# Feed-forwards by seven products in four of eight pairs, with four summed tiles and a fixed TensorE order

## The chip, the core and the metric

The kernel runs on one core of a Trainium2 chip. The metric is the device time of one execution in microseconds (us); the time before is the median of three runs. The engines are TensorE (PE in the profile; its weight loads are PEld), VectorE (DVE), ScalarE (ACT), GpSimd (POOL) and SyncE (SP), which only starts DMA transfers. Each has a queue of its own that it works through in order, and they meet by semaphores.

## The reference

One layer of an encoder on 256 tokens of width 2048, all in float32: a first feed-forward, a mixing layer (convolution and spatial gating side by side), cross-attention into 256 memory tokens, a second feed-forward, and a final norm. The change concerns the feed-forwards:

```python
def swiglu_ffn(h, w_in, w_out):
    gate, up = jnp.split(h @ w_in, 2, axis=-1)
    return (jax.nn.silu(gate) * up) @ w_out

h = rms_norm(x, ffn1_norm)
x = x + 0.5 * swiglu_ffn(h, ffn1_w_in, ffn1_w_out)
...
h = rms_norm(x, ffn2_norm)
x = x + 0.5 * swiglu_ffn(h, ffn2_w_in, ffn2_w_out)
```

`w_in` is 2048 x 11264 and `w_out` 5632 x 2048.

## The kernel before

**Numbers in two parts.** Every matmul is in fp32r. Both factors are split into a rounded high part and the remainder, the low part, and three matmuls are made: high x high, high x low, low x high. The activations are split once. Each weight tile (128 x 1024, 512 KB) is split as it comes: a load by SP's queue into a `raw` buffer, a cast on ScalarE (L397, the high part), a subtraction on VectorE (L398, the low part), both into a buffer `hl`. `parts` does this for the feed-forwards, with three rotating `hl` buffers and two more called `ring` (three in the first feed-forward, one of them called `more`).

**Groups.** The first product of a feed-forward, h @ w_in, goes in 11 groups of 512 gate and 512 up columns (`NG` is 11). Group 0 is written out in `run`; groups 1 to 10 call `group`. A group runs over 16 tiles k of 128 rows, taken as 8 pairs p (tiles 2p and 2p+1). A pair is a 256 x 256 by 256 x 1024 product, cut in two each way, and it is done in one of two ways, which `PATTERNS` spells:

- `C`, by `eight`: eight block products of 128 x 128 by 128 x 512, so 24 matmuls (`by_two` makes 12 for each tile).
- `S`, by `seven`: seven block products of sums and differences, as in Strassen's scheme, so 21 matmuls (`three` makes the 3 of one product). It needs sums of weight blocks, which VectorE makes (L470, L471, L477, L484), and sums of activation blocks, the `forms`, made once by `sides` in group 0. Its products are issued in the order 5, 7, 6, 1, 2, 3, 4. Their weights are split in four steps: `sums` for 5 and 7, the first tile for 6 and 1, the second tile for 2 and 3, and 512 columns more for 4.

The pattern is SCSCSCCC: three pairs by seven.

**Banks.** A group takes all eight PSUM banks, one for each product name 1 to 7 and one, 8, that only the `C` pairs use. When the last `S` pair of a group is done, `joins_sevens` adds products 1, 5, 6 and 7 into four SBUF accumulators: ScalarE copies bank 1 (L521) and VectorE makes four additions (L522 to L525). These free the banks 5, 7, 6 and 1, with which the next group begins. Products 2, 3, 4 and 8 gather on through the `C` pairs; at the end of the group VectorE adds them (L550, four times) and `give` applies the silu on ScalarE (L510) and the products on VectorE (L512).

**Summed tiles.** To spare VectorE, some tiles of `C` pairs get their low part in another way (`summed`): the raw tile is loaded, ScalarE writes the negative high part (L426) and the high part (L427), and a DMA from POOL's queue adds the raw tile from HBM onto the negative high part (L428). `SUMMED` names them: tiles 2, 7 and 13 of a group. Their raw load stands in SP's queue (L425). Two buffer sets alternate (`hl_s` and `more`, or two called `hl_s`); from group 8 of the second feed-forward on there is one, and the tiles are 2 and 10 (`ALONE`). The next tile of a buffer set is begun right after the cast that follows the tile's use (`self.next`).

**Other parts.** The product with `w_out` of the first feed-forward is done by `out_block`, with the same `seven` and `eight`. `turn` makes four transposes on TensorE and splits what they give, so that the result of the first product can be used by the second.

**What sets the order.** The program is written in source order. A planner takes it to pieces at build time: it goes through a modelled timeline and gives each engine the order of its instructions, by when they can run, so products of different pairs may be mixed. `tc.issue_after(ins)` ties what is issued inside its block, on the engine of `ins` alone, behind `ins` in that engine's order.

Of the kernel before, what the change touches and what calls it, by code (L numbers as in the profile page):

```python
# [36 lines left out]
PATTERNS = ("SCSCSCCC", "SCSCSCCC")  # L37

SUMMED = ((2, 7, 13), (2, 7, 13))
ALONE = (2, 10)  # L40

# [37 lines left out]
def layer(ctx: ExitStack, tc: tile.TileContext, a: dict):  # L79
# [220 lines left out]
    def turning(o, c, sink):  # L300

        def go():
            tp = pa.tile([P, 2, T], F32, name="aux")
            for k in range(2):
                for t in range(2):
                    nc.tensor.transpose(  # L306
                        out=tp[:, k, t * P:(t + 1) * P], in_=o[:, t, c + k * P:c + (k + 1) * P], identity=ident
                    )
            sink(tp)
        return go  # L310
# [5 lines left out]
    def three(acc, x, hi, lo, first, last):  # L316

        nc.tensor.matmul(acc, lhsT=x[0], rhs=hi, start=first, stop=False)  # L318
        nc.tensor.matmul(acc, lhsT=x[0], rhs=lo, start=False, stop=False)  # L319
        nc.tensor.matmul(acc, lhsT=x[1], rhs=hi, start=False, stop=last)  # L320

    def by_two(acc, x, hi, lo, k, first, last):

        cols = [slice((g + 1 - k % 2) % 2 * G, (g + 1 - k % 2) % 2 * G + G) for g in range(2)]
        for t in range(2):
            s = slice(t * P, (t + 1) * P)
            for g in range(2):  # L330
                nc.tensor.matmul(acc[t][g], lhsT=x[:, 0, s], rhs=hi[:, cols[g]], start=(t, g) in first, stop=False)  # L331
                nc.tensor.matmul(acc[t][g], lhsT=x[:, 0, s], rhs=lo[:, cols[g]], start=False, stop=False)  # L332
            for g in range(2):
                nc.tensor.matmul(acc[t][g], lhsT=x[:, 1, s], rhs=hi[:, cols[g]], start=False, stop=last)  # L334
# [7 lines left out]
    class FeedForward:  # L342
# [6 lines left out]
        def __init__(self, stack, tags, x_hl, gain, w_in, pattern, summed, w_out=None, pair=False):  # L349
# [34 lines left out]
            self.next = None  # L384
# [34 lines left out]
        def summed(self, at):  # L419
# [5 lines left out]
            nc.sync.dma_start(out=raw, in_=self.w_in[j, :, k])  # L425
# [38 lines left out]
        def seven(self, j, p, b, last):  # L464

            k = 2 * p
# [19 lines left out]
            three(b["4"], self.half(j, k + 1, 1), w[:, 0, lo], w[:, 1, lo], self.begins("4"), False)  # L486
# [5 lines left out]
        def eight(self, j, p, b, last, plain, between=None):  # L492
            for k in (2 * p, 2 * p + 1):
# [7 lines left out]
                by_two(acc, self.x(j, k), w[:, 0], w[:, 1], k, begin, last and k % 2 == 1)  # L501
# [18 lines left out]
        def joins_sevens(self, b, p1, u2, u4, u5):  # L520
            nc.scalar.copy(out=p1, in_=b["1"])  # L521
# [3 lines left out]
            nc.vector.tensor_tensor(out=u5, in0=u2, in1=b["5"], op=ALU.add)  # L525

        def group(self, j, r, after=()):
# [8 lines left out]
            n = len(self.pattern)  # L536
            for p, c in enumerate(self.pattern):
                if c == "S":
                    self.seven(j, p, b, p == self.spairs[-1])
                    if p == self.spairs[-1]:  # L540
                        self.joins_sevens(b, p1, u2, u4, u5)
                else:
                    late = p > self.spairs[-1] and len(after) > 0
                    self.eight(j, p, b, p == n - 1, late)
                    if p > self.spairs[-1] + 1:
# [110 lines left out]
        def turn(self, i):  # L656

            def go():
# [17 lines left out]
                turning(self.h[i // 2], i % 2 * 2 * P, both)()  # L676
# [13 lines left out]
    with ExitStack() as stack:  # L690
# [7 lines left out]
        def x_more(k):  # L698
# [4 lines left out]
            if k in (6, 9, 12):  # L703
                ff.sides(k // 3 - 2)
# [490 lines left out]
    with ExitStack() as stack:  # L1195
# [15 lines left out]
        def first_beside(k):  # L1211
            if k in (6, 9, 12):
                ff.sides(k // 3 - 2)
# [156 lines left out]
```

## Time and profile before

| | us |
|---|---|
| median of three runs | 2089.99 |
| lowest and highest | 2089.42, 2090.06 |
| the profiled execution | 2088.91 |
| its span, first to last instruction | 2087.1 |
| its TensorE busy | 2076.4 |
| its VectorE busy | 1622.5 |
| its ScalarE busy | 1174.4 |

In the profile a row of a timeline gives the start, the busy duration, engine, line, operation, what it writes and reads, the shape and the count; in square brackets stand the idle time before it and what ended that. Durations of instructions that follow each other overlap at their ends, so the time that a row of them takes is read from the distance of their starts. A table by stage gives for each stretch of time how long each engine was busy and with how many instructions. L331 to L334 are the matmuls of `by_two`, L318 to L320 those of `three`.

### The profile page before, as it was taken

How to read it: one execution, taken by the hardware profiler on the slowest of the kernel's cores; microseconds unless marked ns; L12 is line 12 of the kernel's file. 1: busy time of each engine (PE TensorE's matmuls, PEld its weight loads, DVE VectorE, ACT ScalarE, POOL GpSimd, SP SyncE). 2: the span in 40 equal slices, each digit the busy share in tenths (PEclk: the TensorE clock that was granted, in tenths of full speed). 3: DMA queues.
4: the chain of work that ended last, by engine and by line, in shares of the span. 5: the costliest groups of instructions: out<-in, count | busy, mean ns of one | idle time of the engine just before them, and what ended most of it. 6: DMA issues, size and time to landing. Idle time of an engine off the chain costs nothing.

```text
span 2087.1 us, 26730 instructions
## 1 busy us (share of the span) xinstructions
PE 2076.4 (99%) x9765; PEld 1739.0 (83%) x9765; DVE 1622.5 (78%) x2302; ACT 1174.4 (56%) x1470; POOL 66.0 (3%) x81
## 2 busy tenths in 40 slices
PE   9999999999999999999999999999999999999998
PEld 8888888888888888888888899888888888888886
DVE  7888888877777689989877666778888888787754
ACT  8665666555545554445764455566665655554443
POOL 0000000000000000000000000000000000000000
PEclk9999999999999999999999999999999999999999
DMA  9787778755566576655555543687777777556664
GB/s 366 246 263 246 232 223 263 230 182 192 188 203 234 180 238 199 186 179 187 180 196 192 184 160 124 200 291 224 237 236 253 222 217 230 169 166 203 195 192 152
DMA packets 122245, 441.30 MB, mean 211 GB/s; under 512 B 13569, under 2 KB 13953, under 8 KB 121729
## 3 DMA queue, kind: packets, MB, share of 16 engines
q1 hardware_dynamic: 113184, 407.08, 57.1%
q0 software_dynamic: 8352, 31.46, 8.1%
q8 instruction: 76, 1.25, 0.2%
q10 hardware_dynamic: 576, 1.06, 0.1%
q14 instruction: 57, 0.46, 0.1%
HBM read 437.44 MB, written 2.10 MB: 211 GB/s over the span
## 4 chain that ended last, share of the span: by engine, by line
PE 87%; issue 11%; POOL 1%; DMA 1%; ACT 0%; DVE 0%; DVEq 0%; POOLq 0%
PE acc L332 11%; PE acc L331 11%; PE acc L334 11%; PE acc L204 8%; PE acc L205 8%; PE acc L203 8%; PE acc L154 8%; PE acc L162 4%; PE acc L318 3%; PE acc L319 3%; PE acc L320 3%; PE aux L306 1%; PE aux L318 1%; PE aux L319 1%; PE aux L320 1%
## 5 line engine op out<-in xcount | busy, mean ns | idle before, releaser
L124 ACT CAST hl<-raw 128x1024 fp32r<-128x1024 f32 (+1 forms) x315 | 327.1, 1040 | 358.9 <-PE acc L205 191.9
L125 DVE TENSOR_TENSOR hl<-raw,hl 128x1024 fp32r<-128x1024 f32 (+1 forms) x315 | 381.2, 1212 | 165.0 <-ACT hl L124 163.6
L397 ACT CAST hl<-raw 128x1024 fp32r<-128x1024 f32 (+1 forms) x151 | 147.6, 988 | 117.3 <-PE acc L334 48.2
L398 DVE TENSOR_TENSOR hl<-raw,hl 128x1024 fp32r<-128x1024 f32 (+1 forms) x151 | 172.2, 1145 | 47.4 <-ACT hl L397 45.7
L398 DVE TENSOR_TENSOR hl<-spare,hl 128x1024 fp32r<-128x1024 f32 (+1 forms) x125 | 144.7, 1162 | 32.5 <-ACT hl L397 30.3
L397 ACT CAST hl<-spare 128x1024 fp32r<-128x1024 f32 (+1 forms) x125 | 124.3, 1002 | 66.4 <-PE acc L334 24.2
L332 PE MATMUL acc<-hl,x_hl 128*128 128x512 f32 x388 | 140.9, 390 | 0.1
L331 PE MATMUL acc<-hl,x_hl 128*128 128x512 f32 x388 | 135.7, 390 | 0.0
L334 PE MATMUL acc<-hl,x_hl 128*128 128x512 f32 x388 | 120.6, 390 | 0.0
L397 ACT CAST ring<-spare 128x1024 fp32r<-128x1024 f32 (+1 forms) x83 | 82.1, 993 | 59.6 <-issue 19.1
L398 DVE TENSOR_TENSOR ring<-spare,ring 128x1024 fp32r<-128x1024 f32 (+1 forms) x83 | 95.2, 1150 | 20.3 <-ACT ring L397 19.6
L332 PE MATMUL acc<-ring,x_hl 128*128 128x512 f32 x276 | 101.3, 389 | 0.0
L204 PE MATMUL acc<-hl,x_hl 128*128 128x512 f32 x256 | 100.7, 393 | 0.0
L204 PE MATMUL acc<-hl,m_hl 128*128 128x512 f32 x256 | 100.4, 392 | 0.0
L205 PE MATMUL acc<-hl,m_hl 128*128 128x512 f32 x256 | 100.3, 392 | 0.0
L205 PE MATMUL acc<-hl,x_hl 128*128 128x512 f32 x256 | 100.0, 391 | 0.0
L331 PE MATMUL acc<-ring,x_hl 128*128 128x512 f32 x276 | 98.6, 390 | 0.0
L203 PE MATMUL acc<-hl,m_hl 128*128 128x512 f32 x256 | 90.9, 392 | 0.0
L203 PE MATMUL acc<-hl,x_hl 128*128 128x512 f32 x256 | 90.2, 392 | 0.0
L334 PE MATMUL acc<-ring,x_hl 128*128 128x512 f32 x276 | 86.2, 389 | 0.0
L332 PEld LDWEIGHTS acc<-hl,x_hl 128*128 128x128 f32 x388 | 72.6, 188 | 15.5 <-DVE hl L133 0.4
L334 PEld LDWEIGHTS acc<-hl,x_hl 128*128 128x128 f32 x388 | 72.9, 188 | 15.1
(518 smaller groups left out, 5100.8 us busy)
## 6 DMA issues: line engine op xcount, KB each, us to landing
spare<-in_ffn_w_in SPq DMA_DIRECT2D x184, 512.0 KB, 6.8
raw<-in_ffn_w_in SPq DMA_DIRECT2D x157, 512.0 KB, 5.9
raw<-in_ffn_w_out SPq DMA_DIRECT2D x138, 512.0 KB, 4.0
hl_s<-in_ffn_w_in POOLq DMA_DIRECT2D x42, 512.0 KB, 8.3
raw<-in_w_mix_vg SPq DMA_DIRECT2D x32, 512.0 KB, 4.3
raw<-in_w_k SPq DMA_DIRECT2D x32, 512.0 KB, 3.6
raw<-in_w_v SPq DMA_DIRECT2D x32, 512.0 KB, 4.0
raw<-in_w_mix_out SPq DMA_DIRECT2D x32, 512.0 KB, 4.4
```

Source lines behind the costliest of these rows:

```text
L124: nc.scalar.copy(out=hl[:, 0, :size], in_=raw[:, :size])
L125: newest[0] = nc.vector.tensor_tensor(out=hl[:, 1, :size], in0=raw[:, :size], in1=hl[:, 0, :size].bitcast(F32), op=ALU.subtract)
L154: done = nc.tensor.matmul(acc, lhsT=hi[:, k], rhs=xs[k], start=first and k == 0, stop=last and k == kk - 1, skip_group_check=True,)
L162: done = nc.tensor.matmul(acc[:, 0], lhsT=lo[:, k], rhs=xs[k][:, 0], start=False, stop=last and k == kk - 1, skip_group_check=True,)
L203: nc.tensor.matmul(acc[t], lhsT=x[:, 0, s], rhs=hi[:, k], start=k0 + k == 0, stop=False)
L204: nc.tensor.matmul(acc[t], lhsT=x[:, 0, s], rhs=lo[:, k], start=False, stop=False)
L205: nc.tensor.matmul(acc[t], lhsT=x[:, 1, s], rhs=hi[:, k], start=False, stop=k0 + k == nk - 1)
L331: nc.tensor.matmul(acc[t][g], lhsT=x[:, 0, s], rhs=hi[:, cols[g]], start=(t, g) in first, stop=False)
L332: nc.tensor.matmul(acc[t][g], lhsT=x[:, 0, s], rhs=lo[:, cols[g]], start=False, stop=False)
L334: nc.tensor.matmul(acc[t][g], lhsT=x[:, 1, s], rhs=hi[:, cols[g]], start=False, stop=last)
L397: self.cast = nc.scalar.copy(out=hl[:, 0, :n], in_=raw[:, :n])
L398: newest[0] = nc.vector.tensor_tensor(out=hl[:, 1, :n], in0=raw[:, :n], in1=hl[:, 0, :n].bitcast(F32), op=ALU.subtract)
```

## The change

Sixteen groups (1 to 9 of the first feed-forward, 1 to 7 of the second) take the pattern SCSCSCSC; group 10 of the first and groups 8 to 10 of the second keep SCSCSCCC, now called `FEWER`. Group 0 of each, `out_block` and all else keep their products. Summed tiles become 2, 6, 10 and 14 (in group 10 of the first feed-forward 2, 6 and 10). Their raw load goes by POOL's queue in place of SP's. Four sets of `forms` are made in group 0, after tiles 4, 7, 10 and 13, where there were three after 6, 9 and 12.

Two ties are new. `tied` puts the matmuls of every pair, by seven or by eight, and the transposes of every `turn` behind the last matmul of the pair or `turn` before (`self.pe`), so these blocks stand in source order on TensorE. And `seven` puts its VectorE work behind the last joining addition made so far (`self.joined`), which is that of the group before.

```diff
-PATTERNS = ("SCSCSCCC", "SCSCSCCC")
-
-SUMMED = ((2, 7, 13), (2, 7, 13))
+PATTERNS = ("SCSCSCSC", "SCSCSCSC")
+
+FEWER = "SCSCSCCC"
+
+SUMMED = ((2, 6, 10, 14), (2, 6, 10, 14))
 ALONE = (2, 10)
+
+SIDES = (4, 7, 10, 13)
...
-            nc.sync.dma_start(out=raw, in_=self.w_in[j, :, k])
+            nc.gpsimd.dma_start(out=raw, in_=self.w_in[j, :, k])
             nc.scalar.activation(out=hl[:, 1], in_=raw, func=AF.Copy, scale=-1.0)
             nc.scalar.copy(out=hl[:, 0], in_=raw)
             nc.gpsimd.dma_start(out=hl[:, 1], in_=self.w_in[j, :, k], accum_op=ALU.add)
...
+        def tied(self):
+
+            return nullcontext() if self.pe is None else tc.issue_after(self.pe.ins)
...
         def seven(self, j, p, b, last):
 
+
+            with self.tied(), nullcontext() if self.joined is None else tc.issue_after(self.joined.ins):
+                self.seven_products(j, p, b, last)
...
-            three(b["4"], self.half(j, k + 1, 1), w[:, 0, lo], w[:, 1, lo], self.begins("4"), False)
+            self.pe = three(b["4"], self.half(j, k + 1, 1), w[:, 0, lo], w[:, 1, lo], self.begins("4"), False)
...
-                by_two(acc, self.x(j, k), w[:, 0], w[:, 1], k, begin, last and k % 2 == 1)
+                with self.tied():
+                    self.pe = by_two(acc, self.x(j, k), w[:, 0], w[:, 1], k, begin, last and k % 2 == 1)
...
-            nc.vector.tensor_tensor(out=u5, in0=u2, in1=b["5"], op=ALU.add)
+            self.joined = nc.vector.tensor_tensor(out=u5, in0=u2, in1=b["5"], op=ALU.add)
...
-            n = len(self.pattern)
-            for p, c in enumerate(self.pattern):
+            pattern = FEWER if j == NG - 1 or self.pair and j > 7 else self.pattern
+            n, done = len(pattern), pattern.rindex("S")
+            for p, c in enumerate(pattern):
...
-            self.sums_at = [(j, k) for j in range(1, NG) for k in sums if j < NG - 1 or k < min(14, sums[-1])]
+            self.sums_at = [(j, k) for j in range(1, NG) for k in sums if j < NG - 1 or k < 13]
...
-                turning(self.h[i // 2], i % 2 * 2 * P, both)()
+                with self.tied():
+                    self.pe = turning(self.h[i // 2], i % 2 * 2 * P, both)()
...
-            if k in (6, 9, 12):
-                ff.sides(k // 3 - 2)
+            if k in SIDES:
+                ff.sides(SIDES.index(k))
```

More of the change, by code (lines that the diff above doesn't have):

```diff
@@ L319, in three @@
         nc.tensor.matmul(acc, lhsT=x[0], rhs=lo, start=False, stop=False)
-        nc.tensor.matmul(acc, lhsT=x[1], rhs=hi, start=False, stop=last)
+        return nc.tensor.matmul(acc, lhsT=x[1], rhs=hi, start=False, stop=last)
     def by_two(acc, x, hi, lo, k, first, last):
@@ L333, in by_two @@
             for g in range(2):
-                nc.tensor.matmul(acc[t][g], lhsT=x[:, 1, s], rhs=hi[:, cols[g]], start=False, stop=last)
+                done = nc.tensor.matmul(acc[t][g], lhsT=x[:, 1, s], rhs=hi[:, cols[g]], start=False, stop=last)
+        return done
     def bank(pool, name):
```

20 lines of the change are left out of this document (11 added, 9 removed).

## The prediction

> **What bounds the kernel now.** I read the page's busy table first, then what TensorE waited for, then a table by stage, then the timeline of one group of the second feed-forward.
>
> ```profile
> span 2087.1 us, 26730 instructions
> PE 2076.4 (99%) x9765; PEld 1739.0 (83%) x9765; DVE 1622.5 (78%) x2302; ACT 1174.4 (56%) x1470; POOL 66.0 (3%) x81
> ```
> ```profile
> PE aux L232 <- DVE ones L229: 1.1, 1, 1.1
> PE acc L332 <- DMA hl_s<-in_ffn_w_in: 0.8, 1, 0.8
> ```
> ```profile
> 0.00:50.00 50.00, 48.87 (x217) 40.92 (x218) 36.99 (x62) 40.94 (x64) 1.73 (x7) 1.00 0.99 376
> ...
> 1493.60:1535.00 41.40, 41.40 (x184) 34.33 (x183) 34.13 (x42) 26.02 (x28) 2.60 (x3) 1.00 0.77 244
> ```
>
> TensorE is busy 99% of the span, and in a group of a feed-forward (last row: stage, its length, then PE, PEld, DVE, ACT and POOL busy, clock, DMA share, GB/s) it is busy for all of 41.40 us at full clock. In the whole execution it is shown waiting for another engine twice, 1.9 us together. VectorE is next with 34.13 of 41.40. So time falls only if TensorE gets fewer matmuls, and only as long as VectorE still delivers each weight tile (high part by ScalarE, low part by VectorE) ahead of its matmul.
>
> **The price of a matmul.** The busy durations overlap; the distance of starts is what counts.
>
> ```profile
> 1528.47 0.39 PE L331 MATMUL acc<-hl_s,x_hl 128*128 128x512 f32 x1
> ...
> 1531.19 0.39 PE L331 MATMUL acc<-hl,x_hl 128*128 128x512 f32 x1
> ```
>
> These two starts lie one summed tile apart, 12 matmuls: 2.72 / 12 = 0.2267 us each. A pair of weight tiles by eight products is 24 matmuls, 5.44 us; by seven it is 21, 4.76 us.
>
> **What is removed.** One more of the eight pairs goes by seven in groups 1 to 9 of the first feed-forward and 1 to 7 of the second: 16 groups, three matmuls each, 48 x 0.2267 = 10.9 us. All of it lies on the path, since TensorE has no gaps there. A group becomes 180 matmuls, 40.8 us. [...]
>
> **The one late summed tile.** TensorE's second wait is here:
>
> ```profile
> 1698.32 0.86 POOL L428 DMA_DIRECT2D hl_s<-in_ffn_w_in  x1 [27.69 <-ACT hl_s L426]
> ...
> 1707.13 0.50 PE L332 MATMUL acc<-hl_s,x_hl 128*128 128x512 f32 x1 [0.80 <-DMA hl_s<-in_ffn_w_in]
> ```
>
> It is the step from group 7 to 8, where two buffers become one: the buffer of tile 13 of group 7 must serve tile 2 of group 8 only 5.44 + 4.76 = 10.2 us later. With tiles 2, 6, 10, 14 that buffer's last tile before it is 10 of group 7, and 2.72 + 4.76 + 5.44 + 4.76 = 17.7 us lie between. The wait of 0.8 us goes; nothing I find is late next there.
>
> **What VectorE and ScalarE get.** VectorE's and ScalarE's rows at the joint of two groups:
>
> ```profile
> 1526.81 0.68 DVE L525 TENSOR_TENSOR spare<-spare,acc 128x512 f32<-128x512 f32 x1
> 1527.41 0.68 DVE L470 TENSOR_TENSOR spare<-raw 128x512 f32<-128x512 f32 x1
> 1528.01 0.68 DVE L471 TENSOR_TENSOR spare<-raw 128x512 f32<-128x512 f32 x1
> 1528.61 1.22 DVE L398 TENSOR_TENSOR ring<-spare,ring 128x1024 fp32r<-128x1024 f32 x1
> 1529.75 0.68 DVE L477 TENSOR_TENSOR raw<-spare,raw 128x512 f32<-128x512 f32 x1
> 1530.35 1.22 DVE L398 TENSOR_TENSOR hl<-raw,hl 128x1024 fp32r<-128x1024 f32 x1
> 1531.60 0.69 DVE L484 TENSOR_TENSOR raw<-raw,spare 128x512 f32<-128x512 f32 x1
> 1534.81 0.69 DVE L398 TENSOR_TENSOR hl<-raw,hl 128x512 fp32r<-128x512 f32 x1 [2.51 <-ACT hl L397]
> 1535.42 2.48 DVE L550 TENSOR_TENSOR spare<-spare,acc 128x512 f32<-128x512 f32 x4
> 1537.81 0.75 DVE L512 SCALAR_TENSOR_TENSOR h<-spare,r_x,h 128x512 f32<-128x512 f32 x1
> 1538.47 1.22 DVE L398 TENSOR_TENSOR hl<-raw,hl 128x1024 fp32r<-128x1024 f32 x1
> 1539.61 0.75 DVE L512 SCALAR_TENSOR_TENSOR h<-spare,r_x,h 128x512 f32<-128x512 f32 x1
> ```
> ```profile
> 1518.61 0.57 ACT L521 COPY spare<-acc 128x512 f32<-128x512 f32 x1
> ...
> 1530.94 1.06 ACT L426 ACTIVATE hl_s<-spare 128x1024 fp32r<-128x1024 f32 x1 [1.22 <-PE acc L332]
> 1531.90 1.03 ACT L427 CAST hl_s<-spare 128x1024 fp32r<-128x1024 f32 x1
> 1534.15 0.62 ACT L397 CAST hl<-raw 128x512 fp32r<-128x512 f32 x1 [1.22 <-PE acc L334]
> ```
>
> By starts, an operation over 512 columns takes VectorE 0.60 us and a low part over 1024 columns 1.14. A pair by seven is four additions, three long low parts and a short one: 2.40 + 3.42 + 0.61 = 6.43. A pair by eight with one summed tile is one low part, 1.14. The unit of both is 7.57 us of VectorE against 10.20 of TensorE. Per group come the four joining additions (L522 to L525, about 2.6, since three of them wait for the one before), the four closing ones (L550, 2.4) and two products (L512, 1.4): 4 x 7.57 + 6.4 = 36.7 of 40.8 us, 90%. The fourth summed tile a group is what keeps it there; without it, it would be 37.8. ScalarE gains some 2.7 us a group on 26.02. Both fit on average.
>
> **The joint.** What does not fit easily is one place. In the old pattern three pairs by eight (16.3 us) follow the last pair by seven, and the rows show the next group's first pair by seven prepared in them: L470 at 1527.41, while TensorE needs it nearly 9 us later. In the new pattern one pair by eight follows, and the new tie puts all VectorE work of the next seven behind the joining additions. They start when product 1, fourth of the seven, is done. From then TensorE has 9 + 24 matmuls before the next seven, 33 x 0.2267 = 7.48 us, and 18 more plus one before that seven's last low part is read: 11.8 us in all. Until then come ScalarE's copy (0.57), the joins (2.6), the seven (6.43) and three closing additions that free banks 2, 3 and 4 (1.8): 11.4 us. It fits with 0.4 us to spare if nothing else goes ahead. If the fourth closing addition (0.6) and both L512 (1.4) go ahead it is 13.4, a wait of 1.6 us; if ScalarE also takes L426 and L427 (2.0) ahead of the cast for product 6, VectorE's later work waits and I count up to 2.9 us. Below zero it cannot go, as TensorE has no gap there to give up. So this costs 0 to 2.9 us a joint, and there are 16. I take 0.3, near the lower end: the rows show VectorE's order mixed by readiness, a low part slipped between the two L512, which are 1.80 us apart each needing its own ScalarE result first; so part of the closing work should fall behind the next seven. Sum 16 x 0.3 = 4.8 us. This is the weakest number here. After the joint each unit gives VectorE 10.20 - 7.57 = 2.6 us back, so nothing is carried to the next one.
>
> **Summed tiles and their queue.** The rows of the accumulating transfer (duration on POOL, then issue to landing):
>
> ```profile
> L428 POOL DMA_DIRECT2D hl_s<-in_ffn_w_in x42: 854/868/1022, 37.2 to 1795.3; - x42
> DMA to landing us min/median/max: 5.2/8.3/10.0
> ```
> ```profile
> SPq L425 <- ACT hl_s L427: 69.1, 29, 8.4
> ```
>
> With two buffers a tile has 20.4 - 2.72 = 17.7 us from its buffer's release to its use. ScalarE 2.0, POOL 0.87 and 8.3 to 10.0 us to landing make 11.2 to 12.9: 4.8 us to spare, cost 0. POOL's eight issues a group are 7 us of 40.8. A raw load now queues on POOL behind the accumulation of the tile before, which waits for ScalarE, but its own buffer is released no earlier; behind it waits only its own accumulation. On SP the plain loads no longer stand behind L425, which waited there 69.1 us in 29 times; TensorE waits for no plain load now, so that gains nothing.
>
> **The start and the rest.** No wait holds the first raw load on POOL any more, so it can fall into the first microseconds, where DMA is full.
>
> ```profile
> GB/s 45 365 349 365 346 419 413 419 418 407 413 424 419 413 418 419 360 269 413 418 149 221 182 103 274 241 336 419 419 411 303 310 413 136 0 129 269 415 236 0
> ```
>
> At 419 GB/s 512 KB are 1.25 us; TensorE shows no wait for a load there, so I take 0 and keep 1.25. The fourth set of sides gives ScalarE 1.6 and VectorE about 2 us more in the first 50 us, of which they use 40.94 and 36.99: 0, up to 2 if it falls at the end of that stage. TensorE in source order through the second product and the transposes: a transpose's bank is free 1.3 us after it, the next comes 2.7 us on, so 0, up to 2.
>
> **The sum.** The profiled execution took 2088.9 us, span 2087.1 and 1.8 around it; the median of the runs, 2090.0, is 1.1 above it. 2088.9 - 10.9 - 0.8 + 4.8 = 2082.0, as a median 2083.1. A measurement of this kernel can tell about 0.2%, 4.2 us, from no change.
>
> **Rivals.** *The joint eats the gain.* At 0.73 us a joint, 11.7 / 16, gain and wait cancel: 2090. Between 0.47 and 1.0 it stays within 0.2%. For it: VectorE's margin is 0.4 us in 11.8. Against: the tie puts the joins first, as the banks need. Chance 0.15.
>
> *The joint becomes the bound, slower.* If the closing work of a group, older in the source, always goes ahead of the next seven's low parts, TensorE in its tied order cannot take other matmuls meanwhile, as the rows before show it could. At 2.1 us, the middle of 1.3 to 2.9, it is 2078.3 + 16 x 2.1 = 2112; the ends give 2099 and 2125. It decides from 1.0 us on. For it: L550 runs as a block of four at 1535.42. Against: L512 does not. Chance 0.34.
>
> *Summed tiles come late.* If transfers issued by POOL needed 5 us more than the 8.3, each of 64 tiles in the 16 groups would be late as the one at 1707 was: 64 x 0.8 = 51 us, 2129. The row's 854 to 1022 ns, with VectorE busy four fifths of the time, speaks against it. Chance 0.03. [...]
>
> **How the numbers follow.** The forecast's case, joints below 0.47 us, has 0.48, with a range of its own from 2078.3 to 2085.8. Above it the rivals are strung out; the range from 2078 to 2108 leaves out the upper half of the slow case and the late tiles. Faster 0.48, same 0.15, slower 0.37.
>
> **What would show it.** Right: TensorE's groups 40.8 to 41.2 us apart, 48 fewer matmuls, no wait at the step to group 8. Wrong: TensorE waiting for VectorE's low parts (L398) or for ScalarE's cast near L318 to L320 once a group, with groups over 41.5 us; or waits for hl_s.

## The result, and the profile after

The changed kernel takes 2141.78 us (median of five runs, 2140.63 to 2144.00) against 2089.99 before: 1.0251 times, with a 95% interval from 1.0239 to 1.0262. It is slower by 51.8 us, and above the forecast's range, which ends at 2108. Since 48 matmuls and one wait, 11.7 us, did go, the new waits cost 51.8 + 11.7 = 63.5 us.

The page of the changed kernel, its busy table and the first row of its chain of waits, and then that row of the kernel before:

```profile
span 2140.0 us, 26759 instructions
PE 2096.3 (98%) x9717; PEld 1729.6 (81%) x9717; DVE 1672.2 (78%) x2391; ACT 1213.7 (57%) x1525; POOL 121.2 (6%) x171
...
PE 86%; DVE 10%; issue 2%; DMA 1%; ACT 1%; POOL 0%; SPq 0%; DVEq 0%; ACTq 0%
```
```profile
PE 87%; issue 11%; POOL 1%; DMA 1%; ACT 0%; DVE 0%; DVEq 0%; POOLq 0%
```

TensorE has 48 matmuls fewer (9765 before) and yet a longer busy time. Of the chain that ended last, VectorE now holds 10%, where it held 0%. The lines have moved: L323 to L325 are `three`, L336 to L339 `by_two`, L403 and L404 the cast and the low part, L485, L486, L492 and L499 the four additions of a seven, L537 the copy of product 1, L538 to L541 the joining additions, L567 the closing ones and L528 the products with the silu. The four largest of TensorE's waits (line, releaser, total, times, longest) are:

```profile
PE acc L324 <- DVE ring L404: 13.1, 11, 2.4
PE acc L323 <- ACT ring L403: 7.7, 3, 2.6
PE aux L323 <- ACT ring L403: 3.5, 3, 1.2
PE aux L324 <- DVE hl L404: 1.7, 4, 0.9
```

All of them are weights of a seven. The wait for `hl_s` is gone. Now the table by stage for three groups of the first feed-forward and one of the second (columns as before: length, PE, PEld, DVE, ACT, POOL, clock, DMA share, GB/s):

```profile
135.60:179.50 43.90, 42.15 (x182) 33.38 (x181) 37.17 (x47) 27.93 (x31) 5.70 (x8) 1.00 0.81 239
179.50:221.80 42.30, 41.80 (x182) 33.46 (x181) 36.83 (x47) 26.77 (x30) 5.73 (x8) 1.00 0.82 239
221.80:271.50 49.70, 45.24 (x182) 35.27 (x181) 37.50 (x47) 29.07 (x32) 5.67 (x8) 0.93 0.75 219
```
```profile
1572.55:1616.02 43.47, 42.05 (x182) 33.40 (x181) 37.21 (x46) 28.03 (x31) 5.69 (x8) 1.00 0.81 243
```

A group of 180 matmuls should take 40.8 us. In the second feed-forward groups 2 to 7 take 43.5; in the first, 49.2, 43.9, 42.3, 49.7, 43.9, 42.3, 50.0 and 44.0 follow each other. Nine joints there at (3.1 + 1.5 + 8.9) / 3 = 4.5 us and six at 2.7 in the second, and 5.4 at its seventh, from group 7 to 8, make 62 of the 63.5 us. The joint is the place, as the slower rival said. ScalarE's copy of product 1, then VectorE's rows from one joint to the next, second feed-forward:

```profile
1569.76 0.59 ACT L537 COPY spare<-acc 128x512 f32<-128x512 f32 x1 [1.62 <-PE acc L325]
```
```profile
1572.55 0.69 DVE L541 TENSOR_TENSOR spare<-spare,acc 128x512 f32<-128x512 f32 x1
1573.15 0.68 DVE L485 TENSOR_TENSOR spare<-spare 128x512 f32<-128x512 f32 x1
...
1576.09 1.28 DVE L567 TENSOR_TENSOR spare<-spare,acc 128x512 f32<-128x512 f32 x2
...
1580.22 2.35 DVE L404 TENSOR_TENSOR hl<-spare,hl 128x1024 fp32r<-128x1024 f32 x2
1582.49 0.74 DVE L528 SCALAR_TENSOR_TENSOR h<-spare,r_x,h 128x512 f32<-128x512 f32 x1
1583.15 0.68 DVE L404 TENSOR_TENSOR ring<-spare,ring 128x512 fp32r<-128x512 f32 x1
...
1598.39 0.68 DVE L486 TENSOR_TENSOR spare<-spare 128x512 f32<-128x512 f32 x1
1599.69 0.69 DVE L404 TENSOR_TENSOR ring<-raw,ring 128x512 fp32r<-128x512 f32 x1 [0.62 <-ACT ring L403]
...
1609.89 0.69 DVE L404 TENSOR_TENSOR ring<-spare,ring 128x512 fp32r<-128x512 f32 x1 [2.41 <-ACT ring L403]
...
1613.86 0.69 DVE L538 TENSOR_TENSOR spare<-spare,aux 128x512 f32<-128x512 f32 x1 [0.99 <-ACT spare L537]
```
```profile
1582.29 0.39 PE L325 MATMUL acc<-hl,x_hl 128*128 128x512 f32 x1
1583.89 0.50 PE L324 MATMUL acc<-ring,x_hl 128*128 128x512 f32 x1 [1.21 <-DVE ring L404]
```

The brackets carry the story. From the last joining addition (1572.55) VectorE works for 26.5 us without a gap, and TensorE waits in that stretch for the short low part of product 4 (1583.15, released at 1583.89). That one wait is 1.2 of the 2.7 us; the rest are short gaps ahead of it, since the 19 matmuls of the first seven before it take 5.5 us, from 1577.07 on, and not 4.3. After 1599 the same engine stands idle again and again, waiting for casts, which wait for weight buffers, and at last for the copy of product 1: VectorE has run as far ahead as buffers and tie allow. Its average, 37.2 of 43.5 us, shows neither the overfull stretch nor the idle one.

In the long groups the planner put VectorE's fourth addition of the first seven (L499) 11.9 us behind the last joining addition, where it stands at 4.7 in the second feed-forward. Both products with the silu and two additions of the second seven went ahead of it. So ScalarE's cast was late as well, and TensorE also lost clock:

```profile
234.58 0.68 DVE L499 TENSOR_TENSOR raw<-raw 128x512 f32<-128x512 f32 x1
235.29 0.62 ACT L403 CAST ring<-raw 128x512 fp32r<-128x512 f32 x1 [0.17 <-DVE raw L499]
```
```profile
235.96 0.50 PE L323 MATMUL acc<-ring,x_hl 128*128 128x512 f32 x1 [2.58 <-ACT ring L403]
237.65 0.80 PE L324 MATMUL acc<-ring,x_hl 128*128 128x512 f32 x1 [1.19 <-DVE ring L404]
...
239.53 0.63 PE L336 MATMUL acc<-hl_s,x_hl 128*128 128x512 f32 x1
239.95 0.63 PE L337 MATMUL acc<-hl_s,x_hl 128*128 128x512 f32 x1
...
243.55 0.39 PE L336 MATMUL acc<-ring,x_hl 128*128 128x512 f32 x1
243.78 0.39 PE L337 MATMUL acc<-ring,x_hl 128*128 128x512 f32 x1
```

After two waits, 2.58 and 1.19 us, the starts lie 0.42 us apart instead of 0.23, until 243.55. From 237.65 on, 14 matmuls took 5.9 us and not 14 x 0.2267 = 3.2: 2.7 us more, and the stage's clock is 0.93.

### The profile page after: what moved, and what is told of

Same layout as the page of the kernel before. It is cut to its first block, busy times and chain, and to the rows that moved or that the text cites. A ratio compares the mean times of both kernels' runs of the same rounds, so it can differ in the third digit from the quotient of the medians.

```text
span 2140.0 us, 26759 instructions
## 1 busy us (share of the span) xinstructions
PE 2096.3 (98%) x9717; PEld 1729.6 (81%) x9717; DVE 1672.2 (78%) x2391; ACT 1213.7 (57%) x1525; POOL 121.2 (6%) x171
## 4 chain that ended last, share of the span: by engine, by line
PE 86%; DVE 10%; issue 2%; DMA 1%; ACT 1%; POOL 0%; SPq 0%; DVEq 0%; ACTq 0%
PE acc L337 10%; PE acc L336 10%; PE acc L339 10%; PE acc L208 8%; PE acc L209 8%; PE acc L207 8%; PE acc L158 8%; PE acc L166 4%; PE acc L324 3%; PE acc L325 3%; PE acc L323 3%; DVE hl L404 2%; DVE ring L404 2%; DVE spare L567 2%; PE aux L310 1%
## 5 line engine op out<-in xcount | busy, mean ns | idle before, releaser
L404 DVE TENSOR_TENSOR hl<-raw,hl 128x1024 fp32r<-128x1024 f32 (+1 forms) x146 | 169.1, 1162 | 60.0 <-ACT hl L403 57.2
L403 ACT CAST hl<-raw 128x1024 fp32r<-128x1024 f32 (+1 forms) x146 | 145.1, 1003 | 87.6 <-PE acc L339 47.8
L404 DVE TENSOR_TENSOR hl<-spare,hl 128x1024 fp32r<-128x1024 f32 (+1 forms) x141 | 165.7, 1182 | 34.0 <-ACT hl L403 32.3
L403 ACT CAST hl<-spare 128x1024 fp32r<-128x1024 f32 (+1 forms) x141 | 142.2, 1019 | 79.9 <-DVE spare L486 35.4
L337 PE MATMUL acc<-hl,x_hl 128*128 128x512 f32 x372 | 136.1, 390 | 0.3 <-DVE hl L137 0.2
L336 PE MATMUL acc<-hl,x_hl 128*128 128x512 f32 x372 | 131.7, 390 | 0.7 <-ACT hl L403 0.7
L339 PE MATMUL acc<-hl,x_hl 128*128 128x512 f32 x372 | 114.9, 389 | 0.0
L404 DVE TENSOR_TENSOR ring<-spare,ring 128x1024 fp32r<-128x1024 f32 (+1 forms) x81 | 86.9, 1075 | 22.0 <-ACT ring L403 21.5
L208 PE MATMUL acc<-hl,x_hl 128*128 128x512 f32 x256 | 100.6, 393 | 0.0
L209 PE MATMUL acc<-hl,x_hl 128*128 128x512 f32 x256 | 99.9, 390 | 0.0
L403 ACT CAST ring<-spare 128x1024 fp32r<-128x1024 f32 (+1 forms) x81 | 75.2, 931 | 33.5 <-PE acc L325 15.4
L207 PE MATMUL acc<-hl,x_hl 128*128 128x512 f32 x256 | 90.5, 392 | 0.0
L404 DVE TENSOR_TENSOR ring<-raw,ring 128x512 fp32r<-128x512 f32 (+1 forms) x74 | 77.2, 1046 | 16.9 <-ACT ring L403 16.1
L336 PE MATMUL acc<-hl_s,x_hl 128*128 128x512 f32 x216 | 87.3, 404 | 0.0
L337 PE MATMUL acc<-hl_s,x_hl 128*128 128x512 f32 x216 | 87.3, 404 | 0.0
L403 ACT CAST ring<-raw 128x512 fp32r<-128x512 f32 (+1 forms) x74 | 67.0, 909 | 35.0 <-PE acc L325 16.5
L434 POOL DMA_DIRECT2D hl_s<-in_ffn_w_in x54 | 47.2, 873 | 632.8 <-ACT hl_s L432 632.8
```

Source lines behind the costliest of these rows:

```text
L207: nc.tensor.matmul(acc[t], lhsT=x[:, 0, s], rhs=hi[:, k], start=k0 + k == 0, stop=False)
L208: nc.tensor.matmul(acc[t], lhsT=x[:, 0, s], rhs=lo[:, k], start=False, stop=False)
L209: nc.tensor.matmul(acc[t], lhsT=x[:, 1, s], rhs=hi[:, k], start=False, stop=k0 + k == nk - 1)
L339: done = nc.tensor.matmul(acc[t][g], lhsT=x[:, 1, s], rhs=hi[:, cols[g]], start=False, stop=last)
L403: self.cast = nc.scalar.copy(out=hl[:, 0, :n], in_=raw[:, :n])
L404: newest[0] = nc.vector.tensor_tensor(out=hl[:, 1, :n], in0=raw[:, :n], in1=hl[:, 0, :n].bitcast(F32), op=ALU.subtract)
```

## The experiments

My theory after the result was the rival's: VectorE's work behind the joins makes TensorE wait, and the two ties cause it, since VectorE may not prepare the next seven before the joins and TensorE may not take other matmuls while it waits. Against it stood three others: POOL's queue delays the summed tiles; the joint is only short of TensorE work to cover it; VectorE as a whole is too full.

| run | us (median) | ratio to before | 95% interval |
|---|---|---|---|
| changed kernel | 2141.78 | 1.0251 | 1.0239 to 1.0262 |
| e1_no_dve_tie | 2115.21 | 1.0124 | 1.0108 to 1.0141 |
| e2_no_pe_tie | 2129.57 | 1.0191 | 1.0176 to 1.0207 |
| e3_no_ties | 2096.20 | 1.0031 | 1.0020 to 1.0043 |
| e4_raw_by_sp | 2141.06 | 1.0251 | 1.0235 to 1.0266 |
| e9_old_pattern | 2090.35 | 1.0004 | 0.9994 to 1.0013 |
| e5_early | 2165.23 | 1.0361 | 1.0346 to 1.0376 |
| e6_early_no_ties | 2087.53 | 0.9991 | 0.9981 to 1.0001 |
| e10_early_no_pe_tie | 2094.80 | 1.0026 | 1.0015 to 1.0036 |
| e6b_early_no_ties | 2079.84 | 0.9954 | 0.9941 to 0.9966 |
| e12_middle_no_ties | 2093.97 | 1.0021 | 1.0011 to 1.0030 |
| e7_fill | 2149.20 | 1.0284 | 1.0269 to 1.0300 |
| e11_tile2_inside | 2135.36 | 1.0220 | 1.0206 to 1.0234 |
| e13_rest_later | 2134.11 | 1.0219 | 1.0202 to 1.0236 |
| e15_sums_free | 2193.58 | 1.0497 | 1.0481 to 1.0512 |
| e14_more_vector | 2179.36 | 1.0432 | 1.0417 to 1.0448 |
| e16_more_late | 2142.50 | 1.0250 | 1.0232 to 1.0268 |
| e17_low_order | 2122.47 | 1.0156 | 1.0142 to 1.0170 |
| e18_closing_later | 2121.81 | 1.0154 | 1.0140 to 1.0168 |

### Which part of the change: the ties and the queue

```diff
# e1_no_dve_tie
-            with self.tied(), nullcontext() if self.joined is None else tc.issue_after(self.joined.ins):
+            with self.tied():
# e2_no_pe_tie
-            return nullcontext() if self.pe is None else tc.issue_after(self.pe.ins)
+            return nullcontext()
# e3_no_ties: both; e4_raw_by_sp:
-            nc.gpsimd.dma_start(out=raw, in_=self.w_in[j, :, k])
+            nc.sync.dma_start(out=raw, in_=self.w_in[j, :, k])
```

> The changed kernel without the tie of VectorE to the joining additions; TensorE's tie stays. Theory 'joint' (the next group's first seven gets its weight parts too late because all its VectorE work stands behind the joins): additions and first low parts move ahead of the joins, the cost of a joint falls from about 3.9 us to under 1 us, 2085 to 2100 us. Theory 'load' (VectorE at 90% is simply too full) and theory 'TensorE order' (the strict order of the matmuls is the cost): no gain from this edit, 2135 to 2145 us.

> The changed kernel without TensorE's ties; VectorE's tie stays. Theory 'joint': TensorE can put matmuls of the next pair by eight (2.7 us of them are ready from the summed tile) into the wait, which halves it, 2100 to 2125 us. Theory 'TensorE order': the whole loss goes, 2080 to 2090 us. Theory 'load': 2135 to 2145 us.

> The changed kernel without both ties. Theory 'joint': at least as good as the better of the two single edits, 2080 to 2100 us. Theory 'load': above 2120 us.

> The changed kernel with the summed tiles' raw loads back in SP's queue. Theory 'joint': the queue has no part in it, within 5 us of 2142. A theory that the transfers of POOL's queue hold up the tiles: 2100 us or less.

Without VectorE's tie 26.6 us go, without TensorE's 12.2, without both 45.6, which is more than the two single gains together (38.8): each tie makes the other dearer. The single gains fell between the ranges that were expected for them. Of the 17.9 us that are left of 63.5, 16.4 go with other places of the sevens and summed tiles (`e6b_early_no_ties`, below). With one tie left, the wait changes its name. Without VectorE's tie, TensorE in its fixed order waits for banks, since the closing additions (L567) now stand behind the next sevens' work in VectorE's queue:

```profile
PE acc L323 <- DVE spare L567: 20.5, 13, 3.3
```

Without TensorE's tie it waits for casts, and twice for summed tiles:

```profile
PE aux L323 <- ACT hl L403: 12.6, 9, 2.8
PE acc L337 <- DMA hl_s<-in_ffn_w_in: 3.9, 2, 3.0
```

With the raw loads back on SP's queue the time is the same (0.7 us less). POOL's queue has no part in the joints, and its issues stayed at the length that they had before (873 ns each on average, 875 in the kernel before):

```profile
L434 POOL DMA_DIRECT2D hl_s<-in_ffn_w_in x54 | 47.2, 873 | 632.8 <-ACT hl_s L432 632.8
```

### Is it the room behind the joins?

```diff
# e9_old_pattern (ties, POOL's queue and four summed tiles stay)
-PATTERNS = ("SCSCSCSC", "SCSCSCSC")
+PATTERNS = ("SCSCSCCC", "SCSCSCCC")
-SIDES = (4, 7, 10, 13)
+SIDES = (4, 7, 10)
# e5_early
-PATTERNS = ("SCSCSCSC", "SCSCSCSC")
-FEWER = "SCSCSCCC"
-SUMMED = ((2, 6, 10, 14), (2, 6, 10, 14))
+PATTERNS = ("SCSSCSCC", "SCSSCSCC")
+FEWER = "SCSSCCCC"
+SUMMED = ((2, 8, 12, 14), (2, 8, 12, 14))
# e6_early_no_ties: e5 without both ties
# e10_early_no_pe_tie: e5 without TensorE's tie; e6b_early_no_ties: e5 without both; in both:
-            self.sums_at = [(j, k) for j in range(1, NG) for k in sums if j < NG - 1 or k < 13]
+            self.sums_at = [(j, k) for j in range(1, NG) for k in sums if j < NG - 1 or k < 9]
# e12_middle_no_ties: e3 with
+PATTERNS = ("SCSCSSCC", "SCSCSSCC")
+SUMMED = ((2, 6, 12, 14), (2, 6, 12, 14))
```

In `e5_early` and `e6_early_no_ties` tile 12 of the first feed-forward's last group is summed as well, into a buffer that the transposes already write, so that group's values are changed there; the last line of the diff ends that.

> The changed kernel with the pattern of before (SCSCSCCC in all groups, three pairs by seven, sides after tiles 4, 7, 10) and with all the rest of the change: both ties, four summed tiles, their raw loads by POOL's queue. Theory 'joint': 16.3 us of matmuls follow the joins, the ties find room, 2089 to 2094 us. Theory 'TensorE order' (the strict order costs by itself): 2105 us or more.

> The changed kernel with the same four pairs by seven in the same 16 groups and both ties, but placed earlier: pattern SCSSCSCC (SCSSCCCC in the other four groups), summed tiles 2, 8, 12, 14, so that two pairs by eight follow the joins. TensorE then has 57 x 0.2267 = 12.9 us from the joins to the next group instead of 7.48. Theory 'joint': the waits go but for what two sevens in a row cost, 2079 to 2095 us. Theory 'load' (VectorE's work is unchanged, 36.7 us a group): above 2125 us.

> The same early placement without the two ties. Theory 'joint': 2079 to 2092 us, faster than before if the two sevens in a row are kept up with; the ties no longer matter much, within 8 us of the early placement with ties. Theory 'load': as without ties in the late placement, about 2096 us.

> The early placement (SCSSCSCC) with VectorE's tie and without TensorE's; in the last group of the first feed-forward tiles 2 and 8 are summed and not 12. Theory 'lead' (VectorE's lead over TensorE is bounded by the five or six weight buffers, so where it needs more time than TensorE for longer than that lead, TensorE waits unless it has other matmuls to put in): with the order free TensorE fills the waits of the two sevens in a row, 2085 to 2097 us, and VectorE's tie costs under 5 us here because the joins come early. Theory 'VectorE's tie is the cost wherever it stands': 2110 us or more.

> The early placement without both ties; in the last group of the first feed-forward tiles 2 and 8 are summed and not 12. Both theories: as the run of the early placement without ties before, 2085 to 2090 us.

> Four pairs by seven placed SCSCSSCC, summed tiles 2, 6, 12 and 14, no ties. Theory 'lead': two pairs by eight after the joins and TensorE free to fill, 2079 to 2090 us, at least 5 us under the late placement without ties (2096).

With three pairs by eight behind the last seven, both ties, POOL's queue and the fourth summed tile together cost almost nothing (0.4 us more than before, although the wait of the late tile is gone): groups take 41.48 us as 183 matmuls should, although VectorE has 33.6 us of work in them. So a tie is not dear as such. `e5_early` was a miss. It gives the joint two pairs by eight instead of one, and is slower by a further 23 us, because most of the waits moved to the two sevens in a row:

```profile
PE acc L324 <- DVE ring L404: 27.2, 14, 3.4
PE acc L323 <- ACT ring L403: 16.4, 13, 1.7
```

The same pattern without ties is `e6b_early_no_ties`, 2079.84 us. It beats both kernels, and TensorE waits in it for only this:

```profile
PE aux L236 <- DVE ones L233: 1.1, 1, 1.1
PE acc L208 <- DVE hl L129: 0.4, 1, 0.4
```

It comes within 1.6 us of what the prediction's sum gives with joints at nothing (2083.1 - 4.8 = 2078.3). That is better than the 2085 to 2090 that were expected. Ten of the 11.7 us were there to be had, with all of the change but its ties and the places of its sevens and summed tiles. With VectorE's tie kept, the pattern gives 2094.8. `e6_early_no_ties`, which differs in tile 12 of that one group alone, takes 7.7 us more; its expectation that the ties would matter within 8 us in this pattern missed by far, as `e5_early` takes 78 us longer. `e12_middle_no_ties` was a miss too: TensorE waits four times, 7.5 us together, for `hl_s`. By the order of the rows it is tile 2 of the next group: its negative high part is begun only at 1492.21, its accumulating transfer issued at 1493.69, and TensorE goes on with it at 1499.30. What held it back was not followed.

### Cover for the joint, and the clock

`e7_fill` puts twelve matmuls into bank 4 ahead of product 4, which then starts that bank anew. `e11_tile2_inside` moves the twelve of summed tile 2 to the same place, so that nothing is added.

```diff
# e7_fill, in the first seven of groups 2 to 10 (second feed-forward: 2 to 8)
             w = self.parts(two, G)
+            if p == 0 and 1 < j <= (8 if self.pair else NG - 1):
+                fill = self.x_hl[:, 0].rearrange("p two t -> p (two t)")
+                for _ in range(FILL):
+                    nc.tensor.matmul(b["4"], lhsT=self.x_hl[:, 0, 0, :P], rhs=fill, start=True, stop=True)
# e11_tile2_inside, at the same place
+                with self.tied():
+                    self.eight(j, 1, b, False, False, only=2)
```

> The changed kernel with twelve more matmuls (128 x 512, into bank 4 ahead of product 4, which starts that bank anew, so that they leave no result) in the first seven of each group that follows one with four: they work while TensorE would wait. Each costs 0.2267 us, 2.7 us a joint, 43 us in all if nothing waited. If the matmuls after the wait are slow because the granted clock falls after an idle stretch, the groups of 49.7 us in the first feed-forward get shorter and the mean clock goes from 0.993 to 0.998 or more: 2120 to 2140 us. If the clock has no part in it, the groups whose wait is under 2.7 us get longer: 2145 to 2165 us.

> The changed kernel with one thing moved: in each group behind a joint the 12 matmuls of summed tile 2, whose weights need no VectorE, are issued inside the first seven, free to go before or after its product 4, and not behind it. Theories 'joint' and 'lead': the wait ahead of product 4 is filled by up to 2.7 us a joint and the slow clock after it goes with it, 2095 to 2115 us. Theory 'load' (VectorE is full on the whole): the wait comes back later, 2130 to 2145 us.

In `e7_fill` the mean clock rose from 0.993 to 0.998 and two of the three longest groups fell from 49.7 and 50.0 to 47.1 us, although the twelve matmuls take 2.7 us and shorten the wait there only by 1.9 (2.58 to 0.65). So some 3.4 us went with the slow clock in each of these two, near the 2.7 counted from the rows above. The other groups grew (42.3 to 44.2), so the whole became 7 us slower: a miss as a remedy. `e11_tile2_inside` gained 6.4 us, where the joint alone would have given 27 or more; that lies in the range expected for a full VectorE (2130 to 2145). In the second feed-forward its joint no longer waits at product 4, but the second seven does, with VectorE busy without a gap until then:

```profile
1526.20 0.50 PE L323 MATMUL aux<-hl,ring 128*128 128x512 f32 x1 [0.21 <-ACT hl L403]
1542.64 0.50 PE L324 MATMUL acc<-ring,x_hl 128*128 128x512 f32 x1 [2.10 <-DVE ring L404]
```

That felled the plain form of my theory, in which only the first seven is late. The lateness lives in VectorE's queue and is carried on.

### Is VectorE full, or only the stretch behind the joins?

Two runs add the same four VectorE operations (16 x 4 x 0.60 = 38 us over all groups), once in the third seven's sums, once tied behind its last low part.

```diff
# e14_more_vector, ahead of w = self.parts(sums)
+            if p == 4 and j < (8 if self.pair else NG - 1):
+                for _ in range(4):
+                    nc.vector.scalar_tensor_tensor(
+                        out=sums[:, lo], in0=sums[:, lo], scalar=1.0, in1=sums[:, lo], op0=ALU.mult, op1=ALU.max
+                    )
# e16_more_late: the same on two[:, lo], behind w = self.parts(two, G), with
+                with tc.issue_after(newest[0].ins):
```

> Four more operations of VectorE over 512 columns, each on the result of the one before (0.72 us each, 2.9 us in all), in the third seven of each of the sixteen groups, where VectorE's rows show some 6 us of idle time ahead of the joins; they leave the numbers as they are. If only the stretch behind the joins decides, the idle time takes them in: 2137 to 2150. If VectorE's whole work in a group, with an idle time that is forced, decides: 16 x 2.9 = 46 us more, 2175 to 2195.

> The same four operations over 512 columns (16 x 4 x 0.60 = 38 us of VectorE), now behind the third seven's last low part, where VectorE's rows show 5 to 6 us of idle time a group ahead of the joins; the numbers stay as they are. If only the stretch behind the joins, which has no gap, is too full: the idle time takes them in, 2138 to 2150. If every microsecond of VectorE counts, since its idle time is forced by waits on weight buffers that shift along: 2170 to 2185, as where the operations stood in the full stretch.

`e14_more_vector` cost 37.6 us, near the 38 that it adds (46 where each operation waits for the one before, as in the row below). By its expectation that spoke for a full VectorE; but its rows show that the operations had come to stand in the stretch without gaps, 17 to 25 us behind the last joining addition, and not in the idle one. Nor is it a price for that stretch: they also stand ahead of the third seven's first cast, the planner's order around them changed, and its groups became from 2.4 us shorter to 7.7 us longer. `e16_more_late`, where they do stand in the idle stretch, 28 to 41 us behind that addition, cost nothing (2142.50). One row of each, with the last joining addition at 1556.23 and at 1572.31:

```profile
1575.72 2.87 DVE L489 SCALAR_TENSOR_TENSOR spare<-spare 128x512 f32<-128x512 f32 x4
```
```profile
1600.67 0.68 DVE L504 SCALAR_TENSOR_TENSOR raw<-raw 128x512 f32<-128x512 f32 x1
```

VectorE's wait for the copy of product 1, in the changed kernel and then in `e16_more_late`, took the work in:

```profile
DVE spare L538 <- ACT spare L537: 51.3, 17, 5.9
```
```profile
DVE spare L544 <- ACT spare L543: 32.7, 17, 3.8
```

So VectorE as a whole is not too full: 38 us more of its work fit ahead of the joins for nothing. What is left is its order in the stretch behind them, and the next runs change that.

### Taking work out of the stretch

```diff
# e13_rest_later: in the sixteen groups the fourth closing addition and give() wait for the next group's first seven
+                    if self.rest is not None:
+                        with tc.issue_after(newest[0].ins):
+                            self.rest()
# e15_sums_free: L485 and L486 outside the tie, the rest of a seven inside
+            with nullcontext() if self.joined is None else tc.issue_after(self.joined.ins):
             w = self.parts(sums)
# e17_low_order: e13, and VectorE's work of a pair stands behind the last low part of the seven before it
+            w = self.parts(two, G)
+            self.last_low = newest[0]
...
+            return tc.issue_after(self.last_low.ins) if there else nullcontext()
# e18_closing_later: e17, and the other three closing additions stand behind the seven's third addition
+                with tc.issue_after(third.ins):
+                    self.closing()
```

> In the sixteen groups the fourth closing addition and both products with the silu stand behind the next seven's last low part, so only three closing additions stand ahead of it, as the prediction's hand sum of 11.4 us had it. If only the order ahead of the first seven's last low part decides: 0.60 of the fourth addition and 0.66 of one product leave that stretch, 1.3 of the 2.7 us a joint of the second feed-forward go and at least as much in the first, 16 x 1.3 to 2.7 = 20 to 43 us, 2098 to 2122. If the stretch of VectorE's work up to the second seven decides, the work is only moved behind the first seven and the wait comes back at product 4 of the second: 2132 to 2143. If VectorE's work in the whole group decides, no change: 2138 to 2144.

> The first two additions of a seven are free of the tie to the joining additions, all its later VectorE work stays tied. They can fill the idle time ahead of the joins, so 1.2 us a joint leave the stretch behind them for good. If that stretch decides, up to the first or the second seven: 16 x 1.2 = 19 us and some clock, 2105 to 2123. If VectorE's work in the whole group with a fixed idle time decides, the idle time shrinks by the same 1.2 us and the result is the same, 2105 to 2123. If the free additions push other groups' work late in VectorE's order, as without any tie, less: 2123 to 2142.

> As the run with the fourth closing addition and both products behind the next seven, and in the sixteen groups VectorE's work for a pair also stands behind the last low part of the seven before it. Counted by start distances, from the last joining addition to the end of the first seven's last low part VectorE then has 1.2 of first additions, 3 x 1.14 of long low parts, 1.2 of the other two additions, 1.8 of closing additions and the short low part, 0.6: 8.2 us; TensorE needs it 11.8 - 3.4 = 8.4 us after the same point. To the second seven's last low part it is 17.7 of VectorE against 18.6. If only what the planner puts in early made the stretch too full, the waits shrink to the short gaps: groups of 40.8 to 41.5, 2080 to 2096, with the full gain near 2080. If the stretch is too full by what must be in it, or ScalarE's casts are late next: 2110 to 2140.

> As the run before, and the three closing additions (banks 2, 3 and 4) stand behind the third addition of the next group's first seven. After the last joining addition VectorE then makes that addition by 1.2 + 1.14 + 0.6 = 2.9 us and not by 4.1, ScalarE's cast of about 1.1 follows, and TensorE needs it at 8.8 - 3.4 = 5.4. If the middle deadline is all that is left of the joint: groups of 40.8 to 41.7, 2080 to 2100. If banks 2, 3 and 4 now come free too late for products 2 and 3, or the low parts are late again: 2105 to 2125.

`e13_rest_later` gained 7.7 us only. TensorE's waits in one group of it show why (L404 and L405 are the cast and the low part in these kernels):

```profile
1576.74 0.50 PE L324 MATMUL acc<-ring,x_hl 128*128 128x512 f32 x1 [0.21 <-DVE ring L405]
1588.02 0.50 PE L324 MATMUL acc<-ring,x_hl 128*128 128x512 f32 x1 [0.74 <-DVE ring L405]
```

The first seven's wait fell from 1.21 to 0.21, and the second seven has one instead: work that is moved behind the first deadline is still ahead of the second. `e15_sums_free` was a miss, 52 us slower. It does bring two additions ahead of the joins, but the planner then put the second seven's additions into the stretch, 3.5 us behind the joins; the first seven's last low part came 12.3 us after the last join, not 10.6, and TensorE waited 3.52 us a group in the second feed-forward.

`e17_low_order` takes out of the stretch what the planner put there early, and gained 19.3 us, 11.6 more than `e13_rest_later`, which it contains. The waits for low parts in `ring` went from 13.1 us to 1.8, and the next wait came up, for the cast of the sum that VectorE's third addition makes:

```profile
PE aux L323 <- ACT hl L404: 12.1, 13, 2.2
...
PE acc L324 <- DVE ring L405: 1.8, 4, 1.1
```

So the expected end of 2080 was missed, and the other branch, 2110 to 2140 with late casts, came: I had counted VectorE to the last low part of a seven and not to the sums in between. `e18_closing_later` eases that one (12.1 to 7.4 us), gives 2121.81, the same, and its ScalarE rows at a joint show the next one:

```profile
1549.33 1.05 ACT L404 CAST ring<-spare 128x1024 fp32r<-128x1024 f32 x1 [2.12 <-PE acc L325]
1550.28 0.58 ACT L548 COPY spare<-acc 128x512 f32<-128x512 f32 x1
```

The copy of product 1 stands behind a cast that waits for a weight buffer. TensorE started the pair by eight at 1550.67, 0.4 us after the copy; in the changed kernel the copy starts 1.8 us ahead of that pair. So the joins begin 1.4 us later. Putting the copy ahead was not tried, and whether a group by SCSCSCSC can be brought to 40.8 us in a tied order stays open. That the joints of the first feed-forward repeat in threes fits the rotation of its weight buffers, which no run tested: a group makes 20 weight parts, so with six buffers it begins two places further on each time and is back after three groups; in the second feed-forward, with five, every group begins at the same place.

## Why the prediction was wrong

**Right.** 48 matmuls at 0.2267 us and the 0.8 us of the late tile: `e6b_early_no_ties` gets that gain nearly whole. POOL's queue at nothing once the groups run: `e4_raw_by_sp`. The ties at almost nothing by themselves: `e9_old_pattern`; the one on the transposes shows as a wait of 0.9 us (L310). The start, taken as 0, was a little more: in the first 50 us TensorE makes 217 matmuls before, 210 in the changed kernel, 211 in `e6b_early_no_ties` and 215 with the raw loads on SP's queue, so it cost about 1.5 us. The place and the mechanism of the slower rival were right, to the tied TensorE that cannot take other matmuls meanwhile; its price was not, as even 2.9 us a joint gave only 2125.

**The step that failed: "I take 0.3".** Measured were 2.7 us a joint in the second feed-forward (5.4 at the last) and 4.5 on average in the first, so the term was 62 us and not 4.8. Three things were behind it.

- *The choice between the ends.* The hand sum of 11.4 us against 11.8 was kept by a hope, that "part of the closing work should fall behind". In the second feed-forward's rows VectorE ends the first seven's last low part 14.1 us after the copy of product 1 has begun (1569.76 to 1583.83): all four closing additions, one L528 and the low part of the next pair by eight (1.14 us, in no count of mine) go ahead. Without a wait TensorE would want it 11.6 us after the same point, close to the sum's 11.8 (52 matmuls from the start of product 2 at 1569.56, 1581.35). 14.1 - 11.6 = 2.5 of the 2.7 us.
- *"After the joint each unit gives VectorE 10.20 - 7.57 = 2.6 us back, so nothing is carried to the next one".* That is an average. The planner spends what comes back on the additions of the seven after next, ahead of the low part that TensorE needs; `e11_tile2_inside` and `e13_rest_later` show the wait again at the second seven. And VectorE's margin of 4.1 us a group lies ahead of the joins, where the tie makes it useless: `e16_more_late` put 2.4 us of work there for nothing.
- *The bound of 2.9 us.* It had no term for the clock: 2.7 us go with it in each of three joints, on top of waits of 3.8 us and short gaps. But without the clock these joints would still cost some 6 us. The bound let the closing work and two of ScalarE's operations go ahead, and not the additions of the second seven, behind which L499 stood in the long groups.

The evidence that I gave for the low end was VectorE's order in the kernel before, mixed by readiness. That order had 16.3 us of TensorE's work behind the joins to be mixed in; with 5.4 us and a tie it was not the same order. The row nearest to the new joint was the margin of 0.4 us itself, and a margin of 0.4 in 11.8 with every unlisted operation going to one side should have put the middle of the range, 2.1, first. That would have given 2112, the right direction and not yet the size.

## What to carry to other kernels

An engine that is 90% busy (VectorE here, 36.7 us of 40.8 by the prediction's count) has no slack to speak of where its work comes in a lump: count its queue from the point at which it is released to each deadline behind it, with everything that an in-order queue can put ahead, and not only to the last. A tie that forbids an engine to work ahead turns its idle time into loss, so before fixing an order, look where the idle time lies; adding a little work there shows it, once the rows tell where that work came to stand. Where a pattern is wanted that moves more work to a second engine, leave cover for it behind the point of release, or leave the order to readiness.

## What the runs showed of the hardware

In two runs TensorE's clock fell to half behind waits of 2.05 to 2.58 us, for which the forecast had no term. In `e17_low_order` one wait of 2.18 us was followed by starts 0.41 to 0.43 us apart instead of 0.23, for 3.4 us (1519.60 to 1522.99); 0.42 is the distance that the long groups of the changed kernel show at a granted 0.50:

```profile
1518.78 0.51 PE L323 MATMUL aux<-hl,ring 128*128 128x512 f32 x1 [2.18 <-ACT hl L404]
...
1519.60 0.61 PE L324 MATMUL acc<-ring,x_hl 128*128 128x512 f32 x1
1520.01 0.63 PE L325 MATMUL acc<-ring,x_hl 128*128 128x512 f32 x1
1520.43 0.63 PE L323 MATMUL acc<-ring 128*128 128x512 f32 x1
1520.86 0.63 PE L324 MATMUL acc<-ring 128*128 128x512 f32 x1
...
1522.99 0.41 PE L325 MATMUL aux<-hl,ring 128*128 128x512 f32 x1
1523.24 0.40 PE L323 MATMUL acc<-ring,x_hl 128*128 128x512 f32 x1
```

The 2.10 us of `e11_tile2_inside` above were not: the matmuls behind that wait start 0.23 us apart. Nor did the length alone decide in `e17_low_order`, where seven waits of TensorE took 2.05 to 2.19 us. Those that ended at 139.15 (2.05 us), 1518.78 (2.18) and 1649.03 (2.19) were followed by the wider distances, from 1.5 us behind the wait at the latest; those that ended at 270.63 (2.06), 400.87 (2.05), 1605.60 (2.19) and 1735.92 (2.18) were not.

The trace of the changed kernel shows the granted clock itself. Up to TensorE's last matmul it is 0.50 in four stretches: from 99.90, 236.44 and 372.97, for 6.83 us each, and from 1758.78, for 3.41. The starts of the four lie 136.54, 136.53 and 1385.81 us apart, in this trace 40, 40 and 406 times the 3.413 us of the shortest. In the 3.41 us ahead of each start TensorE was busy for 1.43, 0.83, 0.50 and 1.19 us and idle for the other 1.98, 2.58, 2.91 and 2.22. The longest waits that begin in these are three of 2.58 us and one of 2.41; all other waits of TensorE in this run are of 1.21 us or less, and none of those was followed by another such stretch. What decides near 2 us was tested by no run.
